# RMSNorm with repeated rows: one of four row copies of tile 5 moves from GpSimd to ScalarE

## The chip, the cores and the metric

The kernel runs on one core of a Trainium2 chip. The metric is the device time of one execution in microseconds (us); of a kernel that was run several times, the median is given. Lower is better.

## The reference

Each row of `x` is normalised by its root mean square, multiplied by `gamma`, and written out twice in succession.

```python
# x: (8, 512, 2048) f32, gamma: (2048,) f32 -> (8, 1024, 2048) f32
x_rep = np.repeat(x, 2, axis=1)
rms = np.sqrt((x_rep ** 2).mean(axis=-1, keepdims=True) + 1e-6)
x_norm = x_rep / rms
return (x_norm * gamma[None, None, :]).astype(np.float32)
```

The input is 33.5 MB and the output twice that, 67.1 MB.

## The kernel before

**Tiles.** The 4096 rows are cut into eight tiles of 512 rows: 128 partitions with K = 4 rows of 2048 numbers each. A tile in SBUF is `y`, 128 x 8 x 2048 f32, with room for the output. A load (L51, 4 MB) fills the last four of the eight row places; the results go into places 0, 2, 4 and 6; each is then copied into the place after it (`repeat`, L92 to L94); a store (L56, 8 MB) writes out all eight. The pool `rows` has three such buffers, so tile i uses the buffer of tile i - 3, and its load waits until that tile's store has landed.

**Steps of a tile.** The sum of squares of a row comes in one of two ways. `total` (L61 to L65) squares one row on ScalarE into PSUM and accumulates its sum in the same instruction. `square` (L67 to L71) squares several rows on ScalarE into the still unused places of `y`, and `reduce` (L73 to L76) sums them on VectorE. `root` (L78 to L83) makes 1/rms on GpSimd in two small instructions. `scale` (L85 to L90) multiplies each row by its 1/rms and by gamma on VectorE. `repeat` copies, on the engine whose copy it is given; without one it is ScalarE's. `sums` (L153 to L159) is `square` and then `total` of the rows that are summed by row; `mixed` (L161 to L171) takes what `sums` gave and does the rest of a tile, with the store last. It can issue the sums of the next tile (`ahead`) between the root and the scaling.

**Order.** The schedule is manual (L100): every engine executes its instructions in the order in which the program issues them, and all loads and stores are issued on SyncE (SP), on one queue. On SP the order is: loads of tiles 0, 1, 2; stores 0, 1, 2; loads 3, 4, 5; stores 3, 4; loads 6, 7; stores 5, 6, 7.

**Tile 5** is handled apart from the others (L183 to L200). Its four rows are scaled by 1/rms on ScalarE (L190), multiplied by gamma on VectorE in one instruction of four rows (L194), and all four are copied on GpSimd in one instruction (L199, seen in the profile as L94 POOL). Then the store is issued (L200, seen as L56). After it come tile 6, with one row by `total` and three by `square`, and the squares of tile 7, which are issued ahead:

```python
    repeat(5, 0, K, nc.gpsimd.tensor_copy)
    store(5)
    last = mixed(sums(6, 1), by_scalar, ahead=(7, 0))
    mixed(last, shared)
```

Of the kernel before, what the change touches and what calls it, by code (L numbers as in the profile page):

```python
# [9 lines left out]
def kernel(  # L10
# [6 lines left out]
    nc = tc.nc  # L17
# [13 lines left out]
    K = 4  # L31
# [23 lines left out]
    def store(i):  # L55
        nc.sync.dma_start(out=out_t[i], in_=ys[i].rearrange("p j d -> p (j d)"))  # L56
# [4 lines left out]
    def total(i, k, ss):  # L61
        sq = junk.tile([P, D], f32, name="sq")
        nc.scalar.activation(  # L63
            out=sq[:], in_=ys[i][:, x_at + k, :], func=Act.Square, accum_out=ss[:, k : k + 1]
        )  # L65

    def square(i, k0, k1):  # L67

        nc.scalar.activation(  # L69
            out=ys[i][:, k0:k1, :], in_=ys[i][:, x_at + k0 : x_at + k1, :], func=Act.Square  # L70
        )  # L71

    def reduce(i, k0, k1, ss):  # L73
        nc.vector.tensor_reduce(  # L74
            out=ss[:, k0:k1], in_=ys[i][:, k0:k1, :], op=Alu.add, axis=mybir.AxisListType.X
        )  # L76

    def root(k0, k1, ss):  # L78
        at = ss[:, k0:k1]
        nc.gpsimd.tensor_scalar(  # L80
            out=at, in0=at, scalar1=inv_d, scalar2=eps, op0=Alu.mult, op1=Alu.add
        )
        nc.gpsimd.tensor_tensor(out=at, in0=at, in1=power_t[:, k0:k1], op=Alu.pow)  # L83

    def scale(i, k0, k1, rstd):  # L85
        for k in range(k0, k1):
            nc.vector.scalar_tensor_tensor(  # L87
                out=ys[i][:, R * k, :], in0=ys[i][:, x_at + k, :], scalar=rstd[:, k : k + 1],
                in1=gamma_b[:], op0=Alu.mult, op1=Alu.mult,
            )  # L90

    def repeat(i, k0, k1, copy=nc.scalar.copy):  # L92
        y_r = ys[i].rearrange("p (k r) d -> p k r d", r=R)
        copy(out=y_r[:, k0:k1, 1, :], in_=y_r[:, k0:k1, 0, :])  # L94

    def columns():
        return small.tile([P, K], f32, name="ss")
# [52 lines left out]
            repeat(i, k0, k1, copy)  # L150
        store(i)

    def sums(i, by_row):  # L153

        ss = columns()
        square(i, by_row, K)
        for k in range(by_row):
            total(i, k, ss)
        return i, by_row, ss  # L159

    def mixed(given, copies, ahead=None):  # L161
        i, by_row, ss = given
        reduce(i, by_row, K, ss)
        root(0, K, ss)
        if ahead is not None:
            ahead = sums(*ahead)
        scale(i, 0, K, ss)
        for k0, k1, copy in copies:
            repeat(i, k0, k1, copy)
        store(i)  # L170
        return ahead  # L171
# [3 lines left out]
    by_scalar = ((0, H, nc.scalar.copy), (H, K, nc.scalar.copy))  # L175
    by_rows(0, whole)
    two = mixed(sums(1, 1), shared, ahead=(2, 1))
    mixed(two, shared)
    for j in (3, 4, 5):
        new_tile()  # L180
        load(j, 0, K)
    by_rows(3, shared)
    _, _, ss = mixed(sums(4, H), whole, ahead=(5, 0))  # L183
    for j in (6, 7):
        new_tile()
# [10 lines left out]
        in1=gamma_b[:].rearrange("p (k d) -> p k d", k=1).to_broadcast([P, K, D]), op=Alu.mult,  # L196
    )

    repeat(5, 0, K, nc.gpsimd.tensor_copy)  # L199
    store(5)  # L200
    last = mixed(sums(6, 1), by_scalar, ahead=(7, 0))
    mixed(last, shared)


# [28 lines left out]
```

## Time and profile before

| | |
|---|---|
| median of 5 runs | 240.92 us (240.47 to 241.83) |
| the profiled execution | 241.83 us, of which the span is 240.0 us |
| busy: VectorE, ScalarE, GpSimd, TensorE | 133.0, 90.7, 14.7, 7.2 us |
| DMA | 100.67 MB, mean 419 GB/s over the span |
| HBM read, written | 33.56 MB, 67.11 MB |

The span is what the profile shows, from the first to the last instruction; the execution's own time is 1.83 us longer. The profiled execution is the slowest of the five. Engines are named PE (TensorE), DVE (VectorE), ACT (ScalarE), POOL (GpSimd) and SP (SyncE); a "q" behind the name means the engine's instruction queue, so an SPq row is a DMA being issued, not its data. The data are moved by 16 DMA engines, whose packets the trace records one by one. Times in the text are counted from the start of the span.

### The profile page before, as it was taken

The page shows a single profiled execution, that of the slowest core. Times are in us where ns is not written, and L with a number is a line of the kernel's source. Part 1 is how long each engine was busy: PE and PEld are TensorE (multiplying, and loading weights), DVE is VectorE, ACT ScalarE, POOL GpSimd, SP SyncE. Part 2 cuts the span into 40 slices and gives each one's busy share as a digit, 9 for nine tenths or more (in the row PEclk, how much of TensorE's full clock was granted, in tenths as well). Part 3 has the DMA queues.
Part 4 walks back from the last instruction along what each step waited for, and adds up shares of the span by engine and source line. Part 5 has one row for each costly group of instructions (what it writes and reads, how often), then busy time and mean ns, then how long its engine had stood idle before and what let it go on. Part 6 is the DMA issues. An engine that isn't in the chain of part 4 may idle for free. (4 is left out here: it accounts for less than half of the span.)

```text
span 240.0 us, 245 instructions
## 1 busy us (share of the span) xinstructions
PE 7.2 (3%) x8; PEld 2.3 (1%) x8; DVE 133.0 (55%) x45; ACT 90.7 (38%) x47; POOL 14.7 (6%) x20
## 2 busy tenths in 40 slices
PE   0650000000000000000000000000000000000000
PEld 0200000000000000000000000000000000000000
DVE  0049997997930000039979993193087997960000
ACT  2671956500600000198994004800748960500000
POOL 0000001002000000000020002006402002000000
DMA  7999999898989899999989898969999999898984
GB/s 262 433 442 437 437 437 524 349 524 349 524 349 513 360 399 426 420 426 431 508 360 513 360 513 360 513 273 437 437 426 426 448 393 481 360 513 360 513 360 175
DMA packets 2462, 100.67 MB, mean 419 GB/s; under 512 B 279, under 2 KB 285, under 8 KB 286
## 3 DMA queue, kind: packets, MB, share of 16 engines
q1 hardware_dynamic: 2462, 100.67, 98.0%
HBM read 33.56 MB, written 67.11 MB: 419 GB/s over the span
## 5 line engine op out<-in xcount | busy, mean ns | idle before, releaser
L87 DVE SCALAR_TENSOR_TENSOR y<-y,ss,gamma_b 128x2048 f32<-128x2048 f32 x28 | 64.7, 2345 | 10.4 <-POOL ss L83 7.4
L74 DVE TENSOR_REDUCE ss<-y 128x3 f32<-128x6144 f32 (+2 forms) x6 | 41.4, 6903 | 11.0 <-ACT y L69 11.0
L69 ACT ACTIVATE y<-y 128x6144 f32<-128x6144 f32 (+2 forms) x6 | 33.6, 5604 | 26.4 <-DMA y<-in_x_dram 26.4
L63 ACT ACTIVATE sq<-y 128x2048 f32<-128x2048 f32 x13 | 24.4, 1874 | 43.1 <-DMA y<-in_x_dram 43.0
L94 ACT COPY y<-y 128x4096 f32<-128x4096 f32 x6 | 21.6, 3602 | 30.5 <-DVE y L87 30.5
L140 DVE RECIPROCAL ss<-ss 128x2 f32<-128x2 f32 x4 | 0.6, 162 | 50.0 <-ACT ss L139 50.0
L94 DVE COPY y<-y 128x4096 f32<-128x4096 f32 (+1 forms) x6 | 18.0, 3005 | 0.2
L190 ACT ACTIVATE y<-y,ss 128x2048 f32<-128x2048 f32 x4 | 7.8, 1993 | 18.8 <-POOL ss L83 18.8
L194 DVE TENSOR_TENSOR y<-y,gamma_b 128x8192 f32<-128x8192 f32 x1 | 8.7, 8689 | 9.3 <-ACT y L190 9.3
L80 POOL TENSOR_SCALAR ss<-ss 128x4 f32<-128x4 f32 x6 | 1.2, 195 | 169.8 <-DVE ss L74 169.8
L94 POOL COPY y<-y 128x8192 f32<-128x8192 f32 x1 | 7.0, 7011 | 16.6 <-DVE y L194 16.6
L127 PE MATMUL gamma_b<-gamma_row,ones 1*128 1x512 f32 x8 | 7.2, 1077 | 8.2 <-DMA gamma_row<-in_gamma_dram 8.2
L83 POOL TENSOR_TENSOR ss<-ss,power_t 128x4 f32<-128x4 f32 x6 | 6.1, 1009 | 0.5
L127 PEld LDWEIGHTS gamma_b<-gamma_row,ones 1*128 1x128 f32 x8 | 2.3, 319 | 11.5 <-issue 10.3
L63 ACT ACTIVATION_READ_ACCUMULATOR sq<-y 128x1 f32 x13 | 2.4, 186 | 0.0
L118 ACT ACT_TABLE_LOAD x1 | 1.3, 1283 | 0.7 <-PEq L217 0.7
L139 ACT ACTIVATE ss<-ss,eps_t 128x2 f32<-128x2 f32 x4 | 1.2, 296 | 0.2
L113 POOL MEMSET ones<- 1x128 f32 x1 | 0.2, 196 | 0.3 <-POOLq L217 0.3
L217 POOL MEMSET const-float32-0.0<- 128x1 f32 x1 | 0.1, 99 | 0.2 <-issue 0.2
L217 POOL MEMSET const-bfloat16-1.0<- 128x1 bf16 x1 | 0.1, 102 | 0.0
L217 POOL MEMSET const-uint8-127<- 128x1 uint8 x1 | 0.1, 102 | 0.0
L217 POOL MEMSET const-float32-1.0<- 128x1 f32 x1 | 0.1, 100 | 0.0
(2 smaller groups left out, 0.2 us busy)
## 6 DMA issues: line engine op xcount, KB each, us to landing
y<-in_x_dram SPq DMA_DIRECT2D x7, 4096.0 KB, 39.8
y<-in_x_dram SPq DMA_DIRECT2D x2, 2048.0 KB, 10.0
out_dram<-y SPq DMA_DIRECT2D x8, 25.0
gamma_row<-in_gamma_dram SPq DMA_DIRECT2D x6, 1.0 KB
gamma_row<-in_gamma_dram SPq DMA_DIRECT2D x1, 2.0 KB
```

The costliest lines, as they stand in the source:

```text
L63: nc.scalar.activation(out=sq[:], in_=ys[i][:, x_at + k, :], func=Act.Square, accum_out=ss[:, k : k + 1])
L69: nc.scalar.activation(out=ys[i][:, k0:k1, :], in_=ys[i][:, x_at + k0 : x_at + k1, :], func=Act.Square)
L74: nc.vector.tensor_reduce(out=ss[:, k0:k1], in_=ys[i][:, k0:k1, :], op=Alu.add, axis=mybir.AxisListType.X)
L80: nc.gpsimd.tensor_scalar(out=at, in0=at, scalar1=inv_d, scalar2=eps, op0=Alu.mult, op1=Alu.add)
L83: nc.gpsimd.tensor_tensor(out=at, in0=at, in1=power_t[:, k0:k1], op=Alu.pow)
L87: nc.vector.scalar_tensor_tensor(out=ys[i][:, R * k, :], in0=ys[i][:, x_at + k, :], scalar=rstd[:, k : k + 1], in1=gamma_b[:], op0=Alu.mul ...
L94: copy(out=y_r[:, k0:k1, 1, :], in_=y_r[:, k0:k1, 0, :])
L118: nc.scalar.preload_act_table(Act.Sqrt)
L127: nc.tensor.matmul(gamma_b[:, c0 : c0 + bank], ones[:], gamma_row[:, c0 : c0 + bank], start=True, stop=True)
L139: nc.scalar.activation(out=at, in_=at, func=Act.Sqrt, scale=inv_d, bias=eps_t[:])
L190: nc.scalar.activation(out=ys[5][:, R * k, :], in_=ys[5][:, x_at + k, :], func=Act.Copy, scale=ss[:, k : k + 1])
L194: nc.vector.tensor_tensor(out=y_r[:, :, 0, :], in0=y_r[:, :, 0, :], in1=gamma_b[:].rearrange("p (k d) -> p k d", k=1).to_broadcast([P, K, ...
```

## The change

GpSimd copies three of tile 5's four rows. The fourth is copied by ScalarE. `sums` gets a parameter `between`, a function that it calls after `square` and before `total`; for tile 6 it holds that copy, so that on ScalarE it stands between the squares of tile 6's three rows and the sum of its first row. The store of tile 5 is issued after both copies and waits for both. On SP the order of loads and stores stays as it was.

```diff
-    def sums(i, by_row):
+    def sums(i, by_row, between=None):
 
         ss = columns()
         square(i, by_row, K)
+        if between is not None:
+            between()
         for k in range(by_row):
             total(i, k, ss)
         return i, by_row, ss
...
-    repeat(5, 0, K, nc.gpsimd.tensor_copy)
+
+    repeat(5, 0, K - 1, nc.gpsimd.tensor_copy)
+    six = sums(6, 1, between=lambda: repeat(5, K - 1, K))
     store(5)
-    last = mixed(sums(6, 1), by_scalar, ahead=(7, 0))
+    last = mixed(six, by_scalar, ahead=(7, 0))
     mixed(last, shared)
```

## The prediction

> **What bounds the kernel now.** I read the DMA part of the page first, then the busy times in three stretches, then the issues and waits of SP around tile 5, then the timeline from 158 to 200 us. The page has one DMA queue:
>
> ```profile
> q1 hardware_dynamic: 2462, 100.67, 98.0%
> ```
>
> The stretches say where the missing 2% lies. The last two columns are the DMA share and GB/s; before them is busy time by engine.
>
> ```profile
> core 0: us, PE busy (x) PEld busy (x) DVE busy (x) ACT busy (x) POOL busy (x), PEclk, DMA share, GB/s
> 0.00:2.80 2.80, 0.00 (x0) 0.00 (x0) 0.00 (x0) 1.28 (x1) 0.46 (x7) 1.00 0.41 82
> 2.80:236.60 233.80, 7.20 (x8) 2.32 (x8) 132.95 (x45) 89.41 (x46) 14.23 (x13) 1.00 1.00 430
> 236.60:240.00 3.40, 0.00 (x0) 0.00 (x0) 0.00 (x0) 0.00 (x0) 0.00 (x0) 1.00 0.00 0
> ```
>
> From 2.8 to 236.6 us the DMA engines are busy all the time (1.00), with DVE busy for 57% and ACT for 38% of it. The kernel is bound by its 16 DMA engines, and all idle time of the others is slack. The page's chain that ended last leads back from a DVE copy that ends at 213.8 us and stops at compute; it does not follow the stores that were queued ahead of the last one, so it is no guide here. An edit costs time only if a DMA engine comes to the end of one transfer before the next has been issued. So the question is when store 5 is issued, against when load 7, the transfer before it, runs out.
>
> The timeline there (start, duration, engine, line, what it waited for):
>
> ```profile
> 159.82 0.34 SPq L51 DMA_DIRECT2D y<-in_x_dram  x1
> 164.01 7.01 POOL L94 COPY y<-y 128x8192 f32<-128x8192 f32 x1 [16.64 <-DVE y L194]
> 169.59 5.32 ACT L69 ACTIVATE y<-y 128x6144 f32<-128x6144 f32 x1 [14.36 <-DMA y<-in_x_dram]
> 171.05 0.34 SPq L56 DMA_DIRECT2D out_dram<-y  x1
> 174.82 1.86 ACT L63 ACTIVATE sq<-y 128x2048 f32<-128x2048 f32 x1
> 174.95 6.55 DVE L74 TENSOR_REDUCE ss<-y 128x3 f32<-128x6144 f32 x1 [10.99 <-ACT y L69]
> 176.62 0.19 ACT L63 ACTIVATION_READ_ACCUMULATOR sq<-y 128x1 f32 x1
> 180.99 7.03 ACT L69 ACTIVATE y<-y 128x8192 f32<-128x8192 f32 x1 [4.18 <-DMA y<-in_x_dram]
> 181.66 0.19 POOL L80 TENSOR_SCALAR ss<-ss 128x4 f32<-128x4 f32 x1 [10.64 <-DVE ss L74]
> ```
>
> Load 7 is issued at 159.82. The GpSimd copy ends at 171.02, and store 5 is issued 0.03 us later. Tile 6's squares start at 169.59, when load 6 has landed; tile 7's squares start at 180.99, when load 7 has. Between 176.8 and 180.99 ACT is idle: that gap is what the change uses. In the packet records of the trace the 16 DMA engines finish load 6 between 168.17 and 169.11 us, and load 7 between 178.66 and 180.54. Store 5, issued at 171.05, thus lay ready for 7.6 us before the first engine could take it.
>
> **How far ahead must a store be issued?** The first load is issued at 0.72 us and its first packet starts at 1.73: 1.01 us. Store 4 is a tighter case. It is issued at 137.47, the first engine has finished store 3 at 138.16, a lead of 0.69 us, and the records show the engines partly idle only from 138.19 to 138.42, so its packets start 0.95 us after the issue. I take 1.01 us.
>
> **What the Trainium skill says.** (1) "ScalarE: Activation LUTs", What ACT_TABLE_LOAD costs: an activation with immediate scale and bias takes 186 ns + 0.833 ns per element, and successive ones overlap by about 93 ns. For two rows (4096) that is an estimate of 3.60 us; the trace has
>
> ```profile
> L94 ACT COPY y<-y 128x4096 f32<-128x4096 f32 x6 | 21.6, 3602 | 30.5 <-DVE y L87 30.5
> ```
>
> so it agrees, as does the overlap (the squares end at 174.91, the next starts at 174.82). (2) The same page, Table sets: copy is in every table set, so it forces no table load; the trace has one load in all, with squares, roots and copies after it. (3) "SBUF — State Buffer", Who interferes with whom: only VectorE and GpSimd share SBUF ports, ScalarE has its own. Here the six ACT copies take 3.588 to 3.606 us, with DVE busy beside the later ones, which agrees. (4) "DMA: Bandwidth & Descriptors", Specifications: some 0.6 us to the first byte for a DMA issued by SP. The trace shows 0.95 to 1.01, and the trace decides.
>
> **The change, part by part.**
>
> *GpSimd copies three rows.* One instruction of 7.01 us becomes one of about 3/4 of that, 5.26 us, and ends at 169.3 in place of 171.0. Its worth is nothing: store 5 was not late, and GpSimd's next work (L80) waits until 181.66.
>
> *ScalarE copies one row, behind tile 6's squares.* One instruction is added. The trace has no one-row ACT copy; the two-row one less a row (from squares of 3 and 2 rows: 5.32 - 3.61 = 1.71) gives 1.89 us, and the skill's price 1.892. Bounds: 1.86, the one-row square, and 3.60, the two-row copy. I take 1.89. It waits for L194 as well, done at 163.95. So it runs from 174.82 to 176.71.
>
> *Store 5 waits for it.* The issue moves from 171.05 to 176.71 + 0.03 = 176.74, 5.7 us later. Its data can start at 176.74 + 1.01 = 177.75. The first DMA engine is free at 178.66, so 0.9 us is left there. For the end of the kernel only the last engine counts: it finishes load 7 at 180.54 and stores 5, 6 and 7 at 199.85, 219.17 and 238.49, 19.32 us apiece without a gap. Its slack is 180.54 - 177.75 = 2.8 us. This execution's load 7 was slow, 10.49 us on its first engine, where loads 3 and 4 took 9.68. In one without that hiccup the sum is this: from load 6's last landing (169.11), 0.48 to the squares' start, 5.23 to the copy, 1.89 for it, 0.03 and 1.01, makes 8.64 us, against 9.68 of load 7. **A slack of 1.0 us is then left.** Cost: 0. If the cover were gone, each us beyond it would cost a us.
>
> *What is queued behind.* On SP, behind store 5's wait stand stores 6 and 7 only; store 6 is not issued before 195.90, and no load is held. On ACT, `total` of tile 6 moves by 1.8 us and is done at about 178.6; `root` (L80) needs it together with the DVE reduce, which ends at 181.50, so 2.9 us are left. Tile 7's squares start at 180.99 by the DMA, 2.4 us after ACT is free. DVE's reduce (L74) waits for the squares, which the copy stands behind, so it does not move. Cost: 0.
>
> *Sum:* 0 on the span of 240.0. The profiled execution took 241.83 (1.83 around the span) and is the slowest of five, so I forecast no change against the median, 240.92: **240.9 us.** What a measurement here can tell from no change is about 0.3%, 0.7 us.
>
> **The rivals.**
>
> *Slower: the DMA rings run dry ahead of store 5.* The place is the end of load 7. It begins to cost when the store is issued later than 1.0 us (a clean load 7) to 2.8 us (this one) after 176.74. A copy as long as the upper bound of 3.60 would add 1.7: nothing here, 0.7 us in a clean execution, so 241.6. With another 0.4 for a slower wait on two engines it is 242.0. For it: the lead shrinks from 7.6 us to under 2. Against: six ACT copies within 0.02 us of each other, and a lead of 0.69 us before store 4 that lost next to nothing. Chance 0.10.
>
> *Slower: the copy is not released where it stands*, the store waiting for ACT's next work. Behind `total` (178.6) the last engine would still be fed at 179.7, before 180.54; behind tile 7's squares (188.0) it would get data at 189.1, 8.5 us late: 249.4. Against: the store of tile 6 is issued at 195.90, 0.03 us after the ACT copy that ends at 195.87, with ACT's next instruction not before 206.93; waits go by the very instruction. The changed program's order has the copy between squares and `total`. Chance 0.03.
>
> *Faster: the hiccup in load 7 comes from the work beside it*, and moves with it. Between 175.4 and 178.8 us the packets of 32 KB take up to 2.4 us where 1.21 is usual, as `total` and the reduce start. Without it 10.49 - 9.68 = 0.8 us are gained: 240.1. Against: the same is seen at 87 us, where every engine is idle (nothing busy from 80 to 100). Chance 0.03.
>
> **How the numbers follow.** The hidden copy has 0.84; of it I put 0.79 within 0.3%, 0.03 below and 0.02 above by scatter alone, the five runs before lying between -0.2 and +0.4% of their median. Faster is 0.03 + 0.03 = 0.06, slower 0.02 + 0.10 + 0.03 = 0.15, same 0.79. The range goes from 240.2 (the median less 0.3%) to 242.0 (the first rival's upper end); it leaves out the third rival, the 249.4 and some scatter.
>
> **What would show it.** In the profile after: a GpSimd copy near 5.3 us, an ACT copy of one row near 1.89 at about 174.8, store 5's issue within 0.1 us of its end and about 2 us ahead of the first engine's end of load 7; SP's wait ahead of it ended by ACT; tile 7's squares still started by DMA; a DMA share of 1.00 across 176 to 184. I am wrong if DMA engines idle between load 7 and store 5, if the last engine's stores no longer follow at 19.3 us, or if the median moves by over 0.7 us.

## The result, and the profile after

The changed kernel takes 239.51 us (median of 25 runs, 239.01 to 239.86), the kernel before, run beside it, 240.72 us (46 runs, 239.01 to 241.83). The ratio is 0.9947, with a 95% interval of 0.9937 to 0.9958: **faster by 0.5%, 1.2 us**, and below the range of the prediction. The best run of both is the same 239.01. What the change does is to take away the upper part of the spread: no run of the changed kernel is above 239.9, and 42 of the 46 of the kernel before are.

Nearly everything that was meant to be seen is there. The timeline of the changed kernel around tile 5 (start, duration, engine, line, what it waited for):

```profile
159.06 0.34 SPq L51 DMA_DIRECT2D y<-in_x_dram  x1
163.12 5.30 POOL L94 COPY y<-y 128x6144 f32<-128x6144 f32 x1 [16.64 <-DVE y L196]
168.93 5.32 ACT L69 ACTIVATE y<-y 128x6144 f32<-128x6144 f32 x1 [14.60 <-DMA y<-in_x_dram]
174.16 1.88 ACT L94 COPY y<-y 128x2048 f32<-128x2048 f32 x1
174.29 6.55 DVE L74 TENSOR_REDUCE ss<-y 128x3 f32<-128x6144 f32 x1 [11.24 <-ACT y L69]
175.95 1.87 ACT L63 ACTIVATE sq<-y 128x2048 f32<-128x2048 f32 x1
176.10 0.34 SPq L56 DMA_DIRECT2D out_dram<-y  x1
177.76 0.18 ACT L63 ACTIVATION_READ_ACCUMULATOR sq<-y 128x1 f32 x1
178.65 7.03 ACT L69 ACTIVATE y<-y 128x8192 f32<-128x8192 f32 x1 [0.70 <-DMA y<-in_x_dram]
```

The new copy takes 1.88 us, the GpSimd copy 5.30, and store 5 is issued 0.06 us after the new copy's end. Its lead over the first engine's end of load 7 is 0.83 us, not the about 2 us that were to be seen, because that end itself comes earlier. What is to be noticed is the distance between the two rows of L69. Tile 6's squares start when load 6 has landed, tile 7's when load 7 has: 178.65 - 168.93 = 9.72 us. In the kernel before the same two rows are 180.99 - 169.59 = 11.40 us apart. Load 7 is shorter, and load 7 was not touched by the change.

The two stretches of load 7 on its first DMA engine, first of the kernel before, then of the changed one (last two columns: DMA share, GB/s):

```profile
168.17:178.66 10.49, 0.00 (x0) 0.00 (x0) 3.71 (x1) 7.21 (x3) 2.86 (x1) 1.00 1.01 397
```

```profile
167.24:176.93 9.69, 0.00 (x0) 0.00 (x0) 2.64 (x1) 8.00 (x3) 1.18 (x1) 1.00 1.00 433
```

Both have a DMA share of 1. A packet that takes twice its time counts as busy all along; only the rate shows the loss, 397 in place of 433 GB/s. SP's wait ahead of store 5 now ends by ScalarE. In the page's queue line the share of the 16 engines is 98.3% in place of 98.0%:

```profile
SPq L56 <- ACT y L94: 16.6, 1, 16.6
```

```profile
q1 hardware_dynamic: 2462, 100.67, 98.3%
```

The last DMA engine finishes load 6 at 169.11 and load 7 at 180.54 before, 11.43 us; at 168.48 and 178.21 after, 9.74 us. From there on both kernels go alike, with 19.32 us on that engine for each of the three stores, to 238.49 and 236.17. Of these 2.3 us between the two profiled executions 1.7 are load 7's.

### The profile page after: what moved, and what is told of

It reads as the page before. It is cut to its first block, busy times and chain, and to the rows that moved or that the text cites. A ratio compares the mean times of both kernels' runs of the same rounds, so it can differ in the third digit from the quotient of the medians.

```text
span 237.8 us, 246 instructions
## 1 busy us (share of the span) xinstructions
PE 7.2 (3%) x8; PEld 2.3 (1%) x8; DVE 132.9 (56%) x45; ACT 92.6 (39%) x48; POOL 13.0 (5%) x20
## 3 DMA queue, kind: packets, MB, share of 16 engines
q1 hardware_dynamic: 2462, 100.67, 98.3%
## 5 line engine op out<-in xcount | busy, mean ns | idle before, releaser
L69 ACT ACTIVATE y<-y 128x6144 f32<-128x6144 f32 (+2 forms) x6 | 33.6, 5604 | 23.5 <-DMA y<-in_x_dram 23.5
L94 ACT COPY y<-y 128x4096 f32<-128x4096 f32 (+1 forms) x7 | 23.5, 3358 | 31.8 <-DVE y L87 31.8
L94 POOL COPY y<-y 128x6144 f32<-128x6144 f32 x1 | 5.3, 5304 | 16.6 <-DVE y L196 16.6
```

The source lines that it names most:

```text
L69: nc.scalar.activation(out=ys[i][:, k0:k1, :], in_=ys[i][:, x_at + k0 : x_at + k1, :], func=Act.Square)
```

## The experiments

**Theory 1:** a store that lies queued behind a load makes the load's last packets longer; the change helps because it issues store 5 so late that load 7 has no packet left to start. **Theory 2:** the gain comes from the split of the copy itself. **Theory 3:** load 7's slow packets have another cause in that place.

### Same split, store early

```diff
-    six = sums(6, 1, between=lambda: repeat(5, K - 1, K))
+    repeat(5, K - 1, K)
+    six = sums(6, 1)
```

> The changed kernel with the one-row ScalarE copy moved ahead of tile 6's squares. The split of the copy is the same (three rows GpSimd, one row ScalarE), only store 5 is issued early again, near 169.3 us (when GpSimd's three rows are done), some 8 us before load 7 runs out. Theory 1, a store that lies queued behind a load makes the load's last packets longer: time as before, about 240.7, load 7 near 10.5 us on its first engine with 32 KB packets of 1.4 to 2.4 us in its last two rounds. Theory 2, the gain comes from the split itself (a shorter GpSimd copy, no work beside load 7's end): as the changed kernel, about 239.5, packets of 1.21 us.

Measured: 240.92 us, ratio to the kernel before 1.0003 (0.9987 to 1.0018). The split is worth nothing. Store 5 was issued at 168.30; load 7 took 10.13 us on its first engine and 10.72 on its last:

```profile
167.26:177.39 10.13, 0.00 (x0) 0.00 (x0) 3.56 (x1) 7.21 (x3) 1.01 (x1) 1.00 1.01 414
```

Theory 2 falls.

### GpSimd alone, store later by extra copies

The kernel before, with row 0 of tile 5 copied n more times ahead of the copy; ScalarE copies nothing of tile 5. The other engines' work is as before.

```diff
+    for _ in range(n):
+        repeat(5, 0, 1, nc.gpsimd.tensor_copy)
     repeat(5, 0, K, nc.gpsimd.tensor_copy)
```

> The kernel before with GpSimd's copy of row 0 of tile 5 made two times more, ahead of the four-row copy, so that its end and store 5's issue come 3.6 us later, near 174.7; ScalarE copies nothing of tile 5. Theory 1: the store is queued about as load 7's second-last packets start, so part of the loss is gone: 239.6 to 240.3. Theory 2 (split): nothing gained, 240.7.

> The kernel before with GpSimd's copy of row 0 of tile 5 made three times more, so that store 5 is issued near 176.5, as late as in the changed kernel, with more GpSimd work and none on ScalarE. Theory 1: as the changed kernel, about 239.5, load 7 at 9.7 us and packets of 1.21 us to its end. Theory 2 (split): nothing gained, 240.7 or more.

Measured: n = 2, issue at 173.95, 240.89 us, 1.0003 (0.9992 to 1.0014). n = 3, issue at 176.06, 239.35 us, **0.9953 (0.9935 to 0.9971)**. More useless GpSimd work, and the whole gain of the change. With n = 3 the stretch of load 7 is

```profile
167.33:177.01 9.68, 0.00 (x0) 0.00 (x0) 2.96 (x1) 7.21 (x3) 8.65 (x2) 1.00 1.00 433
```

at the full rate, with GpSimd busy for 8.65 us of it. So what counts here is when the store is issued, not which engine copies. For n = 2 the expectation under theory 1 was wrong: I had expected a part of the gain, and there was none.

Two steps beside these fix the edges: half a copy of row 0 more than n = 2 (the lines below are added to that kernel), and n = 4.

```diff
+    half = ys[5].rearrange("p (k r) d -> p k r d", r=R)
+    nc.gpsimd.tensor_copy(out=half[:, 0:1, 1, : D // 2], in_=half[:, 0:1, 0, : D // 2])
```

> The kernel before with two and a half more GpSimd copies of row 0 of tile 5, so that store 5 is issued near 174.9 us: between the 173.95 that brought nothing and the 176.06 that brought 1.2 us. Theory 1a, what matters is whether the store reaches the rings (0.95 us after the issue, so 175.9) before load 7's last packets start on an engine (175.6 and later): only some engines are slowed, 239.4 to 240.2. Theory 1b, any store issued more than about 1 us ahead of the load's end costs the whole: 240.7. Theory 2 (the split of the copy, already contradicted) would say 240.7 too.

> The kernel before with four more GpSimd copies of row 0 of tile 5, so that store 5 is issued near 178.0 us, after the first DMA engine has finished load 7 (177.0) and about when the last has (177.9). By the lead of 1.0 us from issue to first packet every engine idles, the last one by about 1.0 us: 239.4 + 1.0 = 240.4, the rival of the prediction in which the rings run dry. Theory 1 has no other cost here: load 7's packets all 1.21 us. If the lateness were hidden: 239.4.

Measured: with two and a half, issue at 175.09, 240.28 us, 0.9977 (0.9962 to 0.9993), between the two; single runs go from 238.95 to 242.02. With n = 4, issue at 178.08, 240.52 us, 0.9991 (0.9980 to 1.0003). There the DMA engines do run out of work (the rings of the prediction run dry). In stretches of the run with n = 4:

```profile
176.50:177.00 0.50, 0.00 (x0) 0.00 (x0) 0.50 (x1) 0.01 (x1) 0.50 (x1) 1.00 0.30 131
177.00:178.90 1.90, 0.00 (x0) 0.00 (x0) 1.90 (x1) 0.00 (x0) 1.05 (x1) 1.00 0.04 17
178.90:180.00 1.10, 0.00 (x0) 0.00 (x0) 1.10 (x1) 1.00 (x1) 0.00 (x0) 1.00 2.24 953
```

Packets are counted where they start, so a single short stretch says little; but in 1.9 us next to none starts (17 GB/s), and all engines start store 5 between 178.9 and 179.1, the first of them 0.84 us after its issue.

The packet records show how the loss arises. Each line is one DMA engine, with start:duration in ns of load 7's last packets (32 KB, 1213 usual) and S for the first packet of store 5 (64 KB, 2418). The run with two and a half copies, whose store can reach the engines at about 176.0:

```
174.77:1213 175.98:1213 177.19:2418S
174.96:1215 176.17:1219 177.39:2422S
174.11:1213 175.32:1213 176.53:1626 178.16:2418S
174.52:1213 175.73:1725 177.65:1726 179.38:2418S
```

Fourteen of the sixteen engines had started their last load packet by 176.2 and were not slowed, as the first two lines. The other two had one left to start, and were; the last line's packet before that, begun at 175.73, was slowed as well. The very last came to store 5 at 179.38, 2 us behind most, and it sets the end. In the run with the early store (e1) every engine is like the last two, with final packets of 1.35 to 2.25 us; in the kernel before the last two packets of most engines are slow, up to 2.4 us; in the run with n = 3 all are of 1.21 to 1.22.

Taken together, by the lead of store 5's issue over the first engine's end of an undisturbed load 7 (its end of load 6 + 9.68 us):

| kernel | lead, us | load 7, last engine, us | ratio to before |
|---|---|---|---|
| same split, store early | 8.6 | 10.72 | 1.0003 |
| before | 6.8 | 11.43 | 1 |
| n = 2 | 2.9 | 11.15 | 1.0003 |
| n = 2.5 | 1.8 | 10.91 | 0.9977 |
| n = 3 | 0.95 | 9.68 | 0.9953 |
| changed | 0.8 | 9.74 | 0.9947 |
| n = 4 | -1.1 | 9.68, then a gap | 0.9991 |

Lead and load 7 are from one profiled execution of each kernel, the ratio is from all its runs, and the profiled one need not be typical: the kernel before's, 241.83 us, is the slowest of its 46, the early store's, 239.97, one of the fastest of its 14. From 1.8 us up, the loss does not follow the lead: a store issued 8.6 us ahead lengthened load 7 less than one issued 2.9 us ahead.

The best lead is about the 0.84 to 1.0 us from the start of an issue to its first packet, less than the 1.21 us of one load packet: the store arrives while the last packet is under way.

### A quarter of the store early

```diff
-    repeat(5, 0, K - 1, nc.gpsimd.tensor_copy)
+    repeat(5, 0, 1, nc.gpsimd.tensor_copy)
+    flat = ys[5].rearrange("p j d -> p (j d)")
+    nc.sync.dma_start(out=out_t[5][:, : R * D], in_=flat[:, : R * D])
+    repeat(5, 1, K - 1, nc.gpsimd.tensor_copy)
...
-    store(5)
+    nc.sync.dma_start(out=out_t[5][:, R * D :], in_=flat[:, R * D :])
```

> The changed kernel with store 5 cut in two: GpSimd copies row 0 first and a store of its two output rows (2 MB of 8) is issued near 165.5 us, behind load 7 in the queue; the other 6 MB are issued near 176.1 as in the changed kernel. If any store queued behind the load has the whole cost: 240.4 to 240.9, as before. If the cost goes by how much is queued: about 239.8. If only what is issued last matters: 239.5.

```profile
165.05 0.34 SPq L204 DMA_DIRECT2D out_dram<-y  x1
175.89 0.34 SPq L207 DMA_DIRECT2D out_dram<-y  x1
```

Measured: 241.13 us, 1.0014 (1.0000 to 1.0029); load 7 10.88 us on its last engine. A quarter of the store in the queue has the whole cost, though the rest came as late as in the changed kernel. The cutting itself is not the cause: after load 7 the two parts took 19.36 us together, against 19.32 for a whole store.

### A load queued behind a store

The same could hold at the other change of direction, from store 4 to load 6: in the changed kernel ten of store 4's last packets took 2.53 to 3.45 us in place of 2.42. Three runs hold loads back there, the first made from the kernel before, the others from the changed one; the last also holds load 3 back. In each, the loads of tiles 6 and 7 are moved behind tile 5's scalings (L190 of the kernel before), and the load waits for a write of one element into its buffer.

```diff
+    new_tile()
+    nc.scalar.copy(out=ys[6][:, x_at, 0:1], in_=eps_t[:])
+    load(6, 0, K)
```

> The kernel before with load 6 issued late: a ScalarE copy of one element into its buffer, behind the four scalings of tile 5, holds it back from 140.5 to about 155.5 us, when store 4 is in its last packets (these start at 155.3 in the trace of before). Load 7 follows it. Theory 1, extended to a load queued behind a store: store 4's last round of packets, 2.8 to 3.5 us in place of 2.42, becomes shorter, 0.3 to 0.7 us gained, about 240.2. If only a store behind a load has this cost: 240.7.

```diff
+    idle = columns()
+    total(5, 0, idle)
+    new_tile()
+    nc.scalar.activation(out=ys[6][:, x_at, 0:1], in_=idle[:, 0:1], func=Act.Copy)
+    load(6, 0, K)
```

> The changed kernel with load 6 held back on ScalarE to about 156.5 us (a sum of squares whose result is used for one element of the buffer alone, behind tile 5's scalings), after store 4's last packets have started (155.3) and about 1 us before they end. Theory 1 extended to a load behind a store: store 4's last packets fall from 2.5 to 3.5 us to 2.42, 0.1 to 0.3 us gained, 239.2 to 239.4. If only a store behind a load has the cost, or if the load comes too late: 239.5 or up to 239.8.

```diff
+        if j == 3:
+            idle = columns()
+            for _ in range(9):
+                total(2, 3, idle)
+            nc.scalar.activation(out=ys[3][:, x_at, 0:1], in_=idle[:, 3:4], func=Act.Copy)
         load(j, 0, K)
```

> The kernel of the run before this one with load 3 held back as well, from 68.9 to about 87.3 us, by nine sums of squares on the idle ScalarE whose results are used for one element alone; store 2's last packets start at 87.1 and run to 89.5 or later. Theory 1 extended: the slow packets at 87 us (13 to 16 of 2.5 to 2.9 us) go, 0.2 us more, 239.0 to 239.2. Otherwise as the run before, or slower by what load 3 comes late.

Measured, in this order: 240.41 us, 0.9995 (0.9977 to 1.0013); 239.70 us, 0.9957 (0.9943 to 0.9971); 240.01 us, 0.9984 (0.9960 to 1.0008). None is better than the kernel it was made from, and the last is, if anything, worse; its single runs go from 239.60 to 242.74. In the second, store 4's last packets did come down to 2.42 us, but load 6's first ones then took 1.3 to 2.6 us in place of 1.21. Here the loss was moved, not removed. Holding back a load behind a store was not worth it.

### The same at another place, with a surprise

These leave work out: tile 3's (or tile 0's) last two rows are not repeated, so that its store is issued 2.2 to 2.5 us earlier.

```diff
-    by_rows(3, shared)
+    by_rows(3, shared[:1])
```

> The changed kernel with part of the work left out: tile 3's last two rows are not repeated (VectorE's copy of 2.3 us), so that store 3 is issued near 114.6 us in place of 116.95, 4.3 us ahead of the first engine's end of load 5 in place of 2.0. Theory 1 (a store queued before an engine starts its last load packets makes these longer), at a place where nothing was changed so far: less work and yet slower than the changed kernel, 240.0 to 240.8, with packets of 1.4 to 2.4 us in the last round or two of load 5 (117.6 and before). Theory 3, that load 7 is special: 239.5, load 5 at 9.69 us.

Measured: 239.52 us, 0.9954 (0.9942 to 0.9967), no different from the changed kernel. The packets did what theory 1 said: 22 of load 5's last packets took 1.3 to 2.15 us, and the load 10.71 us on its last engine (9.72 in the changed kernel). So such packets do not belong to load 7's place: theory 3 falls. But the time came back. Store 4, whose end costs the last engine 0.63 us in the changed kernel (19.95 in place of 19.32), ran in 19.32, and so did load 6 in 9.68. I tried the same on the kernel before, where two early stores should add up:

> The kernel before with the same part of the work left out (tile 3's last two rows are not repeated), so that store 3 is queued early behind load 5 and store 5 early behind load 7. Theory 1 with recovery (an engine that has fallen behind at load 5 loses less at the change from store 4 to load 6, as the trace of the run with the changed kernel showed): both as the kernel before, 240.7, and the load 7 loss of 1.2 us stays since no such change follows it. Plain theory 1 (the losses add up): about 241.8. If the omitted copy itself shortened the kernel and hid a loss: below 240.3.

> The kernel before with the repeat of tile 3's last two rows left out, once more, for a second trace. If the cheap load 7 is regular: load 5 near 10.4 us, load 7 below 10.3 us on its last engine, store 4 at 19.32 us. If it was chance: load 7 at 10.7 us or more.

Measured: 239.57 us, 0.9957 (0.9939 to 0.9974), against every sum of losses; 20 of its 22 runs were below 240.2 and two at 241.5 and 241.9. Store 5 was issued at 170.27, as early as ever, and load 7 took only 10.11 us on its last engine. The second trace, of a single run of 239.85 us, has the same picture, 10.12 us; in the two traces nine and five packets of load 7 take over 1.3 us, against 27 in the kernel before. From load 5 to load 6 the engines' finishing times keep their distances in both traces, 1.05 and 1.16 us from first to last. The rows of L69 for tiles 6 and 7, each waiting for its load, are 10.01 us apart in the first of them (11.40 in the kernel before):

```profile
169.30 5.32 ACT L69 ACTIVATE y<-y 128x6144 f32<-128x6144 f32 x1 [14.86 <-DMA y<-in_x_dram]
170.27 0.34 SPq L56 DMA_DIRECT2D out_dram<-y  x1
179.31 7.03 ACT L69 ACTIVATE y<-y 128x8192 f32<-128x8192 f32 x1 [2.79 <-DMA y<-in_x_dram]
```

Tile 0's early store does not do this:

```diff
-    by_rows(0, whole)
+    by_rows(0, ((0, H, nc.vector.tensor_copy),))
```

> The kernel before with part of tile 0 left out: its last two rows are not repeated, so that store 0 is issued near 27.2 us in place of 29.4, some 4.3 us ahead of the first engine's end of load 2 in place of 2.1: an early store at the first change from loads to stores. Store 5 is early too. If an early store anywhere loses its time once and the engines, once put out of step, pass the later changes more cheaply (what the run before this one suggests): load 2 near 10.5 us, load 7 near 10.0, and the time 239.5 to 240.3, below the kernel before in spite of one more early store. If the losses add up: 241.3 to 242.0. If it is tile 3's place alone that protects load 7: 240.7 or more, with load 7 at 10.7 us or more.

Measured: 240.96 us, 1.0004 (0.9988 to 1.0020). In its timeline the rows of L69 for tiles 1 and 2, each waiting for its load, are 10.56 us apart (9.71 in the kernel before), the loss at load 2:

```profile
22.87 5.32 ACT L69 ACTIVATE y<-y 128x6144 f32<-128x6144 f32 x1 [5.35 <-DMA y<-in_x_dram]
...
26.88 0.35 SPq L56 DMA_DIRECT2D out_dram<-y  x1
...
33.43 5.32 ACT L69 ACTIVATE y<-y 128x6144 f32<-128x6144 f32 x1 [3.35 <-DMA y<-in_x_dram]
```

Store 2, the next one ahead of a load, then ran in 19.32 us without loss; but load 7 took 10.85 us again. The engines lay only 0.6 us apart.

The last run asks whether the distances between the engines are what made the early store 5 cheap. It is tile 3's shortened kernel, made from the kernel before, with load 6 held back as above, which disturbs them.

> The kernel before, with the repeat of tile 3's last two rows left out (store 3 early) and load 6 held back to about 156.9 us as in the run with load 6 late on the changed kernel. If the offsets between the DMA engines, left by the early store 3, are what made the early store 5 cheap: load 6's disturbed first packets undo them, load 7 takes 10.7 us or more on its last engine, time 240.4 to 241.5. If something else about the early store 3 protects load 7: load 7 near 10.1 and 239.4 to 239.9.

Measured: 241.46 us, **1.0043 (1.0023 to 1.0063)**, and load 7 at 10.57 us on its first engine and 10.73 on its last. The same rows are 10.71 us apart:

```profile
169.43 5.32 ACT L69 ACTIVATE y<-y 128x6144 f32<-128x6144 f32 x1 [13.01 <-DMA y<-in_x_dram]
172.01 0.34 SPq L56 DMA_DIRECT2D out_dram<-y  x1
180.14 7.03 ACT L69 ACTIVATE y<-y 128x8192 f32<-128x8192 f32 x1 [3.49 <-DMA y<-in_x_dram]
```

The loss is back, and now it does add up. The same holding back of load 6 had cost nothing on the changed kernel, where store 4 gained what load 6 lost (0.63 and 0.61 us on the last engine). Here store 4 ran in 19.32 us already, so load 6's slow first packets (17 of 1.3 to 2.2 us) are a cost of their own, and part of the 241.46. What these runs show is that an early store's cost depends on what went on at the changes of direction before it. That the engines' distances carry this is argued, not shown: at the end of load 6 they are 1.01 us from first to last here, and 1.04 and 1.16 us in the two traces where load 7 was cheap. If it is the distances, it is the order or the single ones, which were not compared.

## Why the prediction was wrong

**Right, step by step.** The bound (16 DMA engines), the GpSimd copy (5.26 us forecast, 5.30 measured), the ScalarE copy (1.89 and 1.88), its place behind the squares, the issue right behind its end (0.03 and 0.06), SP's wait ended by ScalarE, tile 7's squares still released by the DMA, 19.32 us for each later store. The slack was right too: from load 6's last landing to store 5's first packet the sum had 8.64 us, the trace has 8.6, against 9.68 and 9.74 of load 7; the packet records show partial idling of the DMA engines between load 7 and store 5 that comes to 0.05 us, and the step from n = 3 to n = 4, 2 us later, costs 1.2 us, as the first rival had it. One reading needs a word: the 0.95 to 1.01 us to the first packet are counted from the start of the issuing instruction. From its end, 0.34 to 0.38 us later, the traces have 0.50 to 0.63 us, so they do not contradict the 0.6 us that the prediction set beside them.

**Wrong: one term of the sum, load 7 itself.** The sum held load 7 fixed and asked only whether store 5 came too late. "Its worth is nothing: store 5 was not late" took for granted that a transfer which lies ready early does no harm, and the rule "An edit costs time only if a DMA engine comes to the end of one transfer before the next has been issued" left no place in the sum for a gain. Its being ready early was the loss: 10.49 us for load 7's first engine in place of 9.68, 11.43 for the last. The term was put at 0; it measured -1.2 us by the medians and -1.7 in the profiled pair, in which the kernel before's execution is its slowest.

**The evidence was in the prediction.** It gave load 7's 10.49 us against 9.68 and called it a hiccup of this execution. The third rival even priced its going at -0.8 us, but put it down to work beside it, and gave it 0.03. It was dismissed because slow packets are also seen at 87 us with every engine idle. That is no argument for chance: at 87 us store 2 is in its last packets with load 3 queued behind it, a change of direction as well. I had looked at what the compute engines did, and not at what was next in the queue. And the spread of the five runs (240.47 to 241.83) was read as scatter around a fixed time. The changed kernel's runs cover 0.9 us where the others cover 2.8, which suggests that most of that scatter was this loss, of varying size; one trace of the kernel before cannot show it.

**What stays open.** The runs show when the packets become slow, not what in a DMA engine makes them so. What protects a later change isn't settled either. If it is the engines' distances, their spread alone does not tell: about 1.1 us left by the early store 3 did, 1.0 us after load 6 was held back didn't, nor did 0.6 us left by the early store 0 or 1.2 us in the run with n = 2.

## What to carry to other kernels

A DMA share of 1.00 does not say that the DMA runs at its rate: compare the time of equal transfers, and look at the last packets ahead of each change between loading and storing. In this kernel a store behind a load in a full queue was best issued about one issue-to-first-packet time ahead of the load's end (0.8 to 1.0 us), not as early as possible; useless work that delays it served as well as the change did, and 2 us more of it lost most of the gain again. Before a difference between runs is called scatter, ask which transfer has the same scatter.

## What the runs showed of the hardware that I had not expected

A store queued behind a load made the last one or two packets of the load longer, 1.3 to 2.5 us in place of 1.21 for 32 KB, on those engines that still had a load packet to start; a quarter of the store had the whole cost. Where a load follows a load or a store a store, no more than single slow packets are seen. The losses at several changes of direction do not simply add: with store 3 early as well as store 5 the time was 239.57 us, with load 6 held back besides 241.46. The 16 engines run behind each other at distances that kept their spread for some 50 us, from load 5 to load 6; whether the losses depend on these is not shown.
